# A new order for a two-block layer kernel: loads counted with a longer distance, VectorE's float32 copies kept apart from GpSimd, up to 200 planning rounds

## The chip, the cores and the metric

The kernel runs on one core of a Trainium2 chip. The metric is device time in microseconds (us) of one execution, the median of several runs. TensorE (PE in the profile), VectorE (DVE), ScalarE (ACT) and GpSimd (POOL) each work through a queue of instructions in order; SyncE (SP) issues all transfers between HBM and the on-chip memory SBUF, also in order. PSUM holds the results of matmuls, in 8 banks.

## What is computed

Two layers follow each other over 2048 tokens of width 1024, all in float32. Cut to what matters:

```python
def first_block(x, c, ...):
    shift, scale, gate = split(silu(c) @ ada_w + ada_b, 3)
    h = rmsnorm(x, norm_pre) * (1 + scale) + shift
    proj = h @ w_in                                   # 1024 -> 3072 columns
    attn = sliding_window_attention(q, k, v, sinks) * silu(ag)   # 8 heads, window 128
    rwkv = rwkv7_mixer(h, r, k, v, ...) * silu(rg)    # 4 heads, a recurrence over tokens
    gla = gla_mixer(h, gq, gk, gv, ...) * silu(gg)    # 4 heads, gated linear attention
    y = concat([attn, rwkv, gla]) @ w_out
    return x + gate * rmsnorm(y, norm_post)

def second_block(x, positions, ...):
    h = rms_norm(x, norm_g)
    q, k, v, qi, ki, wi, z_a, u_b, z_b, gates = split(h @ w_in_2)   # 1024 -> 4648
    # each query keeps the 256 best keys by an index score, then softmax over them
    a = dsa_attention(rope(q), rope(k), v, rope(qi), rope(ki), wi, 256) * silu(z_a)
    b = multiscale_pool(u_b, pool_w, pool_scale) * silu(z_b)
    g = sigmoid(gates + merge_bias)
    return x + (g[0] * (a @ w_branch_a) + g[1] * (b @ w_branch_b)) @ w_out_2

def reference(...):
    return second_block(first_block(x, c, ...), positions_2, ...)
```

## The kernel before

**Recording, then planning.** The program first writes down all work as a list of operations. A call such as `nc.vector.tensor_scalar(...)` issues nothing; `Plan.record` notes the operation, the memory that it reads and writes, and from these what it depends on. At the end `Plan.emit` asks `Plan.order` for one order of all operations and issues them in it. That is why every instruction of the profile has the same line, L414. The order fixes each engine's queue and SP's queue of transfers; at run time every engine works through its queue in order and waits for the data of the next instruction.

**The plan's rounds.** `order` starts from a rank for each operation: the length of the longest chain from it to the end. `forward` simulates the five queues: when an engine comes free, it takes the ready operation of highest rank (`walk`). `backward` does the same from the end, and gives new ranks. This goes on for at most `PASSES` rounds, or until `PATIENCE` rounds brought no shorter total; the order with the shortest planned total is kept.

**What the plan counts.** `price` gives the duration of an operation. A transfer is issued every 475 ns, starts 1125 ns after its issue or when the transfer before it is done, and lasts its bytes over 360 bytes per ns. `lag` is the distance from the end of an operation to the start of one that depends on it: some 100 to 240 ns between engines, 900 ns behind a transfer, 100 ns ahead of one. For two operations of one engine whose dependence carries no data it is 0.

**VectorE beside GpSimd.** `port` says of an operation whether VectorE or GpSimd holds the shared way into SBUF while it runs: before, the operations with two inputs in SBUF (`PAIRS`). `until` then lets a holding operation of VectorE start no earlier than 60 ns before the end of GpSimd's holding one, and any operation of GpSimd no earlier than 60 ns before the end of VectorE's. An operation whose start would be put off by more than `WAIT` (150 ns) is put aside for another ready one (`aside`).

**Movable operations.** Copies, scalings and sums in float32 have more than one way (`others`): a copy can run on ScalarE, VectorE or GpSimd. `forward` moves such an operation off its home engine if it is late and the other engine finishes it sooner.

**The work itself.** Tokens are held in four quarters of 512. Every float32 matmul with weights is split in three with high and low parts (`mm3`, `dense_s`). `weights` loads a 128x1024 block of raw weights (in_w_in, in_w_out and so on; 512 KB), splits it on ScalarE and GpSimd, and stores both parts in HBM (scr_w); later uses load the two parts again, 512 KB each. Two buffers of each part take turns. `dense` runs a list of weight tiles over one or two quarters. `mixers` holds the attention, RWKV and GLA work of one half of the tokens, which passes results through HBM (scr_am, scr_lt, scr_xt, scr_yT). `build_h` normalises rows of x or y: its two scalings per pair of rows are VectorE's 128x1024 float32 scalings. `out1`, `proj2_rows`, `topk`, `attn2` and `out2` are the later stages. Work without dependences between stages may run side by side, as the plan has it.

Of the kernel before, what the change touches and what calls it, by code (L numbers as in the profile page):

```python
# [8 lines left out]
F32 = mybir.dt.float32  # L9
F32R = mybir.dt.float32r  # L10
# [8 lines left out]
PSUM = bass.MemoryType.PSUM  # L19
# [18 lines left out]
EJ = ((2, "vector"), (3, "tensor"), (0, "tensor"), (1, "vector"))  # L38
B1, B2, B3, B4, B5 = 1, 1, 1, 1, 1
K0, K1, K2, K3, M0, M1 = 3, 4, 4, 4, 2, 2  # L40
PASSES, PATIENCE = 32, 12
SWITCH, NEAR, LOOK, WAIT, AHEAD = 90.0, 3000.0, 12, 150.0, 60000.0
FLEX, MARGIN, GAIN = 3, -10000.0, 500.0
ENGINES = ("tensor", "vector", "scalar", "gpsimd", "sync")
# [18 lines left out]
class Plan:  # L63
# [118 lines left out]
    def record(self, eng, name, args, kw):  # L182
        o = Op()
        o.eng, o.name, o.args, o.kw = eng, name, args, kw
        o.preds, o.succs, o.more = {}, [], set()
        i = len(self.ops)
        reads, writes = operands(name, args, kw)
        o.cost = price(eng, name, args, kw, reads, writes)
        o.ways = [(eng, name, args, kw, o.cost)]
        o.kind = kind(name, reads) if eng == "tensor" else None  # L190
        o.port = port(name, reads)
        for way in others(eng, name, args, kw, reads, writes):
            o.ways.append((*way, price(*way, reads, writes)))
        for aps, w in ((reads, False), (writes, True)):
            for ap in aps:
                r = self.region(ap)
                if r is not None:
                    self.touch(o, i, r, w and ap.tensor.name not in self.junk, ap.tensor.name)
        o.preds.pop(i, None)
        self.ops.append(o)  # L200
# [89 lines left out]

    def until(self, o, e, t):

        if e == "vector" and o.port:
            return max(t, self.held["gpsimd"] - 60.0)
        if e == "gpsimd":
            return max(t, self.held["vector"] - 60.0)
        return t
# [14 lines left out]
    def forward(self, rank, goal):  # L312

        ops = self.ops
        end, seq, dma = [0.0] * len(ops), [], [0.0]

        def take(i, e, t, now, avail, done):
            o = ops[i]
            free = self.until(o, e, t)
            if len(o.ways) > 1:  # L320
                mine = next(w for w in o.ways if w[0] == e)
                home = o.ways[0][0]
                if e != home:
                    slack = goal - rank[i] - t + MARGIN
                    if slack > 0:
                        return t + slack
                    w = o.ways[0]
                    start = max(now[home], t)
                    start += sum(ops[j].cost for r, j in avail[home] if -r > rank[i] and not done[j])
                    if start + w[4] <= t + mine[4] + GAIN:  # L330
                        return max(start + w[4] - mine[4] - GAIN, t + 50.0)
                o.eng, o.name, o.args, o.kw, o.cost = mine
            o.start = t
            if e == "sync":
                now[e] = t + 475
                dma[0] = o.end = max(dma[0], t + 1125) + o.cost
            else:
                now[e] = o.end = free + o.cost
                if o.port and e in self.held:
                    self.held[e] = o.end  # L340
                if e == "tensor":
                    if o.kind != self.kind:
                        now[e] = o.end = o.end + SWITCH
                    self.kind = o.kind
            end[i] = o.end
            seq.append(i)

        self.walk([len(o.preds) for o in ops],
                  lambda i: [(s, end[i] + lag(ops[i], ops[s], data)) for s, data in ops[i].succs], rank, take)
        return max(end), end, seq  # L350

    def backward(self, end):

        ops = self.ops
        tail, dma = [0.0] * len(ops), [0.0]
        ways = [o.ways for o in ops]
        for o in ops:
            o.ways = [(o.eng, o.name, o.args, o.kw, o.cost)]

        def take(i, e, t, now, avail, done):  # L360
            o = ops[i]
            if e == "sync":
                now[e] = t + 475
                dma[0] = max(dma[0], t) + o.cost
                tail[i] = dma[0] + 1125
            else:
                now[e] = tail[i] = self.until(o, e, t) + o.cost
                if o.port and e in self.held:
                    self.held[e] = tail[i]
                if e == "tensor":  # L370
                    if o.kind != self.kind:
                        now[e] = tail[i] = tail[i] + SWITCH
                    self.kind = o.kind

        self.walk([len(o.succs) for o in ops],
                  lambda i: [(p, tail[i] + lag(ops[p], ops[i], data)) for p, data in ops[i].preds.items()], end, take)
        for o, w in zip(ops, ways):
            o.ways = w
        return tail

    def order(self):

        ops = self.ops
        for i, o in enumerate(ops):
            for j, data in o.preds.items():
                ops[j].succs.append((i, data))
        rank = [0.0] * len(ops)
        for i in reversed(range(len(ops))):
            rank[i] = max((rank[s] + lag(ops[i], ops[s], data) for s, data in ops[i].succs), default=0.0) + ops[i].cost
        best, goal = None, math.inf  # L390
        stale = 0
        for k in range(PASSES):
            total, end, seq = self.forward(rank, goal)
            stale += 1
            if stale > PATIENCE:
                break
            if best is None or total < best[0]:
                stale = 0
                best = total, seq, [(o.eng, o.name, o.args, o.kw, o.cost, o.start, o.end) for o in ops]
            rank = self.backward(end)  # L400
            goal = total
            self.totals.append(total)
        self.total, self.seq, how = best
        for o, h in zip(ops, how):
            o.eng, o.name, o.args, o.kw, o.cost, o.start, o.end = h
        return self.seq
# [73 lines left out]
def operands(name, args, kw):  # L480

    reads, writes = [], []
    for i, x in enumerate(args):
        if is_ap(x):
            w = i == 0 or name == "tensor_tensor_reduce" and i == 7
            (writes if w else reads).append(x)
    for k, x in kw.items():
        if is_ap(x):
            (writes if k in ("out", "accum_out") else reads).append(x)
    return reads, writes  # L490
# [51 lines left out]
         "copy_predicated", "tensor_tensor_reduce"}  # L542


def port(name, reads):

    if name not in PAIRS:
        return False
    return all(reads[i].space != PSUM for i in (0, -1 if name == "scalar_tensor_tensor" else 1))


def kind(name, reads):


    if name == "transpose":
        return "transpose"
    return reads[0].dtype == F32R, reads[0].shape[0] == 128


def width(ap):  # L560
    n = 1
    for d in list(ap.shape)[1:]:
        n *= d
    return n
# [45 lines left out]
def lag(a, b, data):  # L610

    if a.eng == b.eng and not data:
        return 0.0
    if a.eng == "sync":
        return 900.0
    if b.eng == "sync":
        return 100.0
    return LAG[a.eng][b.eng]
# [1717 lines left out]
```

## Time and profile before

| | us |
|---|---|
| median of 3 runs | 3489.16 (3485.51 to 3496.49) |
| profiled execution | 3483.89 |
| its span, first to last instruction | 3482.1 |

The runs lie within 0.3% of each other. The profile comes from one execution; every stretch "A:B" below is in us from the start of its span. TensorE's mean granted clock in it was 0.956 of full speed.

### The profile page before, as it was taken

What the parts mean: (1) busy time and instruction counts of PE and PEld (TensorE: products, weight loads), DVE (VectorE), ACT (ScalarE), POOL (GpSimd) and SP (SyncE); (2) the same over time, 40 slices, a digit from 0 to 9 for tenths busy, and PEclk for the clock granted to TensorE, in tenths of its full rate; (3) what the DMA queues carried; (4) which work ended last, traced back from release to release, by engine and by line L of the source; (5) the groups of instructions that cost most, each with busy time, mean ns of one, the idle gap of its engine ahead of it and who ended that gap; (6) DMA issues with size and microseconds to landing.
All of it is one profiled execution on the core that took longest, in us unless ns stands there. A gap on an engine that the chain in (4) does not pass through costs nothing.

```text
span 3482.1 us, 53683 instructions
## 1 busy us (share of the span) xinstructions
PE 3165.3 (91%) x18258; PEld 2567.1 (74%) x18258; DVE 2399.1 (69%) x5421; ACT 1756.7 (50%) x3458; POOL 1336.7 (38%) x1379
## 2 busy tenths in 40 slices
PE   6899988998898999798999999999999988898988
PEld 5677666776666888787887777777777766777877
DVE  6367966666883656258878888789788687775442
ACT  3122225432123454257776767875786957446330
POOL 2232545441333554443323444353132236353421
PEclk7899989999998999999999999999999999899999
DMA  8477467547547888656644344362322346665656
GB/s 273 170 248 209 157 174 229 167 151 214 150 121 232 256 271 296 214 173 216 212 157 137 134 139 140 132 213 91 120 73 90 121 152 230 226 212 163 212 162 220
DMA packets 453961, 631.69 MB, mean 181 GB/s; under 512 B 83751, under 2 KB 309552, under 8 KB 453430
## 3 DMA queue, kind: packets, MB, share of 16 engines
q1 hardware_dynamic: 453686, 628.26, 56.1%
q8 instruction: 143, 2.34, 0.3%
q14 instruction: 132, 1.08, 0.1%
HBM read 397.31 MB, written 230.82 MB: 180 GB/s over the span
## 4 chain that ended last, share of the span: by engine, by line
PE 38%; DMA 13%; DVE 9%; ACT 6%; issue 4%; POOL 3%; SPq 1%; ACTq 0%; DVEq 0%; POOLq 0%
PE bank L414 38%; DVE arena L414 9%; DMA arena<-scr_w 6%; ACT arena L414 6%; POOL arena L414 3%; DMA arena<-in_w_in 1%; DMA arena<-in_w_out 1%; DMA out<-arena 1%; SPq L414 1%; DMA arena<-scr_y 0%; DMA arena<-scr_q 0%; DMA scr_x<-arena 0%; DMA arena<-scr_p_zb 0%; DMA arena<-in_w_branch_b 0%; DMA arena<-scr_yT 0%
## 5 line engine op out<-in xcount | busy, mean ns | idle before, releaser
L414 PE MATMUL bank<-arena 128*128 128x512 f32 (+8 forms) x18258 | 3165.3, 337 | 312.5 <-DVE arena L414 124.4
L414 PEld LDWEIGHTS bank<-arena 128*128 128x128 f32 (+3 forms) x18258 | 2567.1, 181 | 910.4 <-DVE arena L414 225.2
L414 POOL TENSOR_TENSOR arena<-arena 128x512 fp32r<-128x512 f32 (+16 forms) x1116 | 1240.1, 1127 | 1618.8 <-ACT arena L414 975.3
L414 ACT ACTIVATE arena<-arena 128x512 fp32r<-128x512 f32 (+32 forms) x1195 | 966.7, 824 | 804.4 <-DVE arena L414 421.1
L414 ACT ACTIVATE arena<-bank 128x512 f32<-128x512 f32 (+8 forms) x1423 | 724.4, 550 | 797.6 <-PE bank L414 649.9
L414 DVE TENSOR_TENSOR arena<-arena 128x512 fp32r<-128x512 f32 (+27 forms) x822 | 583.4, 724 | 209.3 <-ACT arena L414 103.6
L414 DVE SCALAR_TENSOR_TENSOR arena<-arena 128x512 f32<-128x512 f32 (+10 forms) x661 | 433.8, 661 | 59.5 <-POOL arena L414 19.3
L414 DVE TENSOR_SCALAR arena<-arena 128x1 f32<-128x1 f32 (+6 forms) x1129 | 272.8, 248 | 168.3 <-ACT arena L414 124.9
L414 DVE TENSOR_SCALAR_CACHE_REDUCE arena<-arena 128x384 int8<-128x384 bf16 (+13 forms) x238 | 351.3, 1476 | 11.9 <-ACT arena L414 6.8
L414 DVE CUSTOM_DVE_ANT_0 arena<-bank,arena 128x512 f32<-128x512 f32 (+3 forms) x448 | 251.7, 565 | 62.6 <-PE bank L414 60.6
L414 DVE TENSOR_TENSOR arena<-bank,arena 128x512 f32<-128x512 f32 (+3 forms) x170 | 95.4, 569 | 181.2 <-PE bank L414 144.3
L414 POOL TENSOR_SCALAR arena<-arena 128x4 f32<-128x4 f32 (+10 forms) x169 | 69.0, 409 | 327.9 <-DVE arena L414 159.1
L414 DVE SCALAR_TENSOR_TENSOR arena<-arena,bank 128x512 f32<-128x512 f32 (+1 forms) x264 | 127.5, 487 | 75.6 <-PE bank L414 42.4
L414 DVE COPY arena<-bank 128x512 f32<-128x512 f32 (+8 forms) x146 | 79.6, 548 | 114.9 <-PE bank L414 106.5
L414 ACT ACTIVATE arena<-bank,arena 128x512 f32<-128x512 f32 (+3 forms) x175 | 99.5, 579 | 65.0 <-PE bank L414 64.2
L414 DVE SCALAR_TENSOR_TENSOR arena<-bank,arena 64x64 f32<-64x64 f32 (+4 forms) x209 | 82.0, 393 | 63.1 <-PE bank L414 48.3
L414 ACT ACTIVATION_READ_ACCUMULATOR arena<-arena 128x1 f32 x590 | 114.9, 195 | 0.0
L414 POOL MEMSET arena<- 64x256 f32 (+7 forms) x69 | 21.8, 319 | 109.9 <-PE bank L414 57.6
L414 DVE CAST arena<-arena 128x512 fp32r<-128x512 f32 (+5 forms) x50 | 37.2, 751 | 24.2 <-PE bank L414 6.3
L414 DVE TENSOR_SCALAR arena<-bank 64x256 f32<-64x256 f32 (+2 forms) x44 | 18.0, 410 | 51.4 <-PE bank L414 47.0
L414 DVE TENSOR_TENSOR_SCAN arena<-arena 128x512 f32<-128x512 f32 (+14 forms) x26 | 53.1, 2041 | 0.2
L414 DVE TENSOR_REDUCE arena<-arena 128x1 f32<-128x3 f32 (+6 forms) x148 | 37.3, 252 | 9.5 <-ACT arena L414 8.1
(18 smaller groups left out, 215.7 us busy)
## 6 DMA issues: line engine op xcount, KB each, us to landing
arena<-scr_w SPq DMA_DIRECT2D x340, 512.0 KB
scr_w<-arena SPq DMA_DIRECT2D x174, 512.0 KB
arena<-in_w_in SPq DMA_DIRECT2D x52, 512.0 KB
arena<-in_x SPq DMA_DIRECT2D x32, 512.0 KB
scr_p_g<-arena SPq DMA_DIRECT2D x64, 256.0 KB
arena<-scr_p_g SPq DMA_DIRECT2D x64, 256.0 KB
arena<-in_ada_w SPq DMA_DIRECT2D x48, 256.0 KB
arena<-scr_p SPq DMA_DIRECT2D x16, 532.0 KB
```

What stands on the lines that cost most here:

```text
L414: ins = getattr(getattr(self.nc, o.eng), o.name)(*o.args, **o.kw)
```

## The change

Three things change in the plan, none in the list of operations.

Every operation that depends on a transfer is counted 2700 ns behind the transfer's end, 900 ns before. This holds for loads, and for stores whose tile is written anew or whose data is loaded again.

`port` is asked for each engine. For VectorE a `tensor_scalar` or `tensor_copy` with one output, wider than one element, with its first input and output in float32 in SBUF, now holds the shared way as well. It is asked with the name that the operation was recorded with: a ScalarE `activation` that the plan moves to VectorE as a copy is not counted.

The rounds go up to 200, and 30 may pass without a shorter total.

```diff
-PASSES, PATIENCE = 32, 12
+PASSES, PATIENCE = 200, 30
...
-        o.port = port(name, reads)
+        o.port = {e: port(e, name, reads, writes) for e in ("vector", "gpsimd")}
...
-        if e == "vector" and o.port:
+        if e == "vector" and o.port[e]:
             return max(t, self.held["gpsimd"] - 60.0)
...
-                if o.port and e in self.held:
+                if e in self.held and o.port[e]:
                     self.held[e] = o.end
...
-def port(name, reads):
+def port(eng, name, reads, writes):
     if name not in PAIRS:
-        return False
+        return eng == "vector" and name in ("tensor_scalar", "tensor_copy") and len(writes) == 1 and width(writes[0]) > 1 \
+            and all(x.space != PSUM and x.dtype in (F32, F32R) for x in reads[:1] + writes)
     return all(reads[i].space != PSUM for i in (0, -1 if name == "scalar_tensor_tensor" else 1))
...
     if a.eng == "sync":
-        return 900.0
+        return 2700.0
```

## Rows read from the trace of the kernel before

**Rows 1.** The page's first lines: span; busy us, share, instructions of each engine.

```profile
span 3482.1 us, 53683 instructions
PE 3165.3 (91%) x18258; PEld 2567.1 (74%) x18258; DVE 2399.1 (69%) x5421; ACT 1756.7 (50%) x3458; POOL 1336.7 (38%) x1379
```

**Rows 2.** TensorE's waits, whole span: us in total, times, longest us.

```profile
PE bank L414 <- DVE arena L414: 124.4, 107, 10.1
PE bank L414 <- ACT arena L414: 78.6, 76, 6.1
PE bank L414 <- DMA arena<-scr_w: 73.7, 52, 11.0
PE bank L414 <- POOL arena L414: 26.2, 41, 1.7
```

**Rows 3.** The page's chain that ended last, by line, shares of the span.

```profile
PE bank L414 38%; DVE arena L414 9%; DMA arena<-scr_w 6%; ACT arena L414 6%; POOL arena L414 3%; DMA arena<-in_w_in 1%; DMA arena<-in_w_out 1%; DMA out<-arena 1%; SPq L414 1%; DMA arena<-scr_y 0%; DMA arena<-scr_q 0%; DMA scr_x<-arena 0%; DMA arena<-scr_p_zb 0%; DMA arena<-in_w_branch_b 0%; DMA arena<-scr_yT 0%
```

**Rows 4.** TensorE's waits for stored weights: 348:1740, then 2784:3482.

```profile
PE bank L414 <- DMA arena<-scr_w: 49.9, 27, 11.0
...
PE bank L414 <- DMA arena<-scr_w: 19.2, 18, 2.4
```

**Rows 5.** Timeline of TensorE: start, us, first of the merged, [idle before, releaser].

```profile
862.15 18.04 PE L414 MATMUL bank<-arena 128*128 128x512 f32 x80 [4.40 <-DMA arena<-scr_w]
...
887.12 13.05 PE L414 MATMUL bank<-arena 128*128 128x512 f32 x45 [4.88 <-DMA arena<-scr_w]
...
1067.89 12.36 PE L414 MATMUL bank<-arena 128*128 128x512 f32 x43 [10.97 <-DMA arena<-scr_w]
...
1437.07 3.33 PE L414 MATMUL bank<-arena 128*128 128x256 f32 x14 [9.59 <-DMA arena<-scr_w]
...
3444.30 15.95 PE L414 MATMUL bank<-arena 128*128 128x256 f32 x131 [0.70 <-DMA arena<-scr_w]
```

**Rows 6.** Loads in the chain, from issue to use: start us, us, what.

```profile
987.57 6.53 DMA arena<-scr_w
...
1427.23 9.70 DMA arena<-scr_w
...
2640.86 4.25 DMA arena<-scr_w
...
3436.53 7.63 DMA arena<-scr_w
```

**Rows 7.** Timeline of SP's queue ahead of the load at 1061.67.

```profile
1050.53 0.41 SPq L414 DMA_DIRECT2D scr_yT<-arena  x1
...
1061.67 0.92 SPq L414 DMA_DIRECT2D arena<-scr_w  x2
```

**Rows 8.** Slices of 10 us: length, each engine's busy us, granted clock, DMA share, GB/s.

```profile
1060.00:1070.00 10.00, 2.11 (x4) 1.34 (x5) 0.00 (x0) 0.00 (x0) 0.00 (x0) 0.52 0.92 284
1070.00:1080.00 10.00, 10.00 (x40) 7.42 (x40) 4.47 (x12) 2.77 (x5) 1.28 (x1) 0.80 0.57 196
```

**Rows 9.** Timeline of VectorE and GpSimd; then groups by form: busy us, mean ns.

```profile
1279.54 0.75 DVE L414 TENSOR_SCALAR arena<-arena 128x1024 f32<-128x1024 f32 x1
1280.81 4.46 POOL L414 TENSOR_TENSOR arena<-arena 128x512 fp32r<-128x512 f32 x2 [3.44 <-ACT arena L414]
1283.20 2.62 DVE L414 TENSOR_SCALAR arena<-arena 128x1024 f32<-128x1024 f32 x1 [1.37 <-DMA scr_x<-arena]
...
2460.08 0.48 DVE L414 TENSOR_SCALAR arena<-arena 128x512 f32<-128x512 f32 x1 [0.48 <-PE bank L414]
...
L414 DVE TENSOR_SCALAR arena<-arena 128x512 f32<-128x512 f32 x67 | 41.4, 628 | 22.1 <-ACT arena L414 18.6 <-PE bank L414 2.1 <-DMA arena<-in_ada_w 1.0
L414 DVE TENSOR_SCALAR arena<-arena 128x1024 f32<-128x1024 f32 x30 | 30.1, 1017 | 13.4 <-POOL arena L414 9.0 <-DMA scr_x<-arena 4.3
```

**Rows 10.** SP's waits on TensorE (total us, times, longest); the page's DMA issues.

```profile
SPq L414 <- PE bank L414: 900.4, 376, 20.3
...
arena<-scr_w SPq DMA_DIRECT2D x340, 512.0 KB
```

More of the change, by code (lines that the diff above doesn't have):

```diff
@@ L367, in take @@
                 now[e] = tail[i] = self.until(o, e, t) + o.cost
-                if o.port and e in self.held:
+                if e in self.held and o.port[e]:
                     self.held[e] = tail[i]
```

## The prediction

> **What bounds the kernel now.** I read the busy times first, then TensorE's waits, the chain that ended last, the waits cut by stage, and at last single stalls. The busy times show one engine that is nearly full: TensorE works 3165.3 us of a span of 3482.1 us, VectorE 2399.1 us and the others less [rows 1]. So only TensorE's idle time, some 317 us, and the reduced clock in part of its work can be won by another order. The waits say who ends this idle time: VectorE 124.4 us, ScalarE 78.6 us, stored weights coming back from HBM (scr_w) 73.7 us, GpSimd 26.2 us [rows 2]. The change speaks to the third directly, to the others only through the order. The chain by line, which can be followed back to 927 us, agrees: behind TensorE (38%) and VectorE (9%) stand the stored-weight loads with 6%, some 209 us of the span, and first-time weight loads (in_w_in, in_w_out) with 1% each [rows 3]. Time in the chain is no idle time of TensorE: most of each load runs beside matmuls.
>
> By stage, 49.9 us of the 73.7 us lie between 348 and 1740 us (mixers beside dense layers), 19.2 us from 2784 us to the end [rows 4] and the remaining 4.6 us in the attention stage between. The first stretch is lumpy. Four waits, of 4.40, 4.88, 10.97 and 9.59 us, are 29.84 us of its 49.9 us [rows 5]; the other 23 average 0.87 us.
>
> **The change part by part.** Every instruction is taken from the same recorded list with the same data dependences. No wait and no DMA is added; what moves is the order on each of the five queues, and for some movable copies the engine. So no duration is removed: the change is worth what the new order does to waits.
>
> *Loads.* The plan counts a 512 KB load as 1.125 us + 524288/360 = 1.456 us + 0.9 us = 3.48 us from issue to user, on an idle queue; after the change 5.28 us. The chain holds 34 pieces of scr_w; of these the shortest is 4.25 us, the longest 9.70 us, the first 6.53 us, the last 7.63 us [rows 6]; and 6% of the span over 34 is a mean of 6.1 us [rows 3]. The old count is below even the shortest piece; the new one lies between the shortest and the mean. So the old plan put users too early on TensorE's in-order queue, and matmuls that were ready stood behind them. With 1.8 us more per load it should place such matmuls first, or send the load sooner.
>
> What that is worth, per wait: no more than the 1.8 us that the plan newly sees. Between 348 and 1740 us that is 20.06 us of short waits plus 4 x 1.8 = 7.2 us, 27.3 us; attention 4.6 us; the end at most 19.2 us, where 18 waits average 1.07 us [rows 4]. To use it there must be other matmuls. In the first stretch mixers and dense layers run side by side, so I take three quarters: 20 us. At the end one stream of weights runs through two buffers with little beside it: half, 9 us. Attention: 2 us. Sum 31 us. Of the four long stalls another 29.84 - 7.2 = 22.6 us is not explained by 1.8 us; they are accidents of the order. At 1061.67 us SP sent the load only after a crowd of small attention loads that began to form at 1050.53 us behind a store of yT [rows 7], while TensorE stood still for 10.97 us [rows 5]. A new order deals these anew; I take a third, 8 us. Bounds for the whole part from below and above: 0 us, if nothing else is ready, to 73.7 us.
>
> A stall also costs clock. In the slice with the 10.97 us wait the granted clock is 0.52, and in the next one, with TensorE busy all 10 us, 0.80, so part of it at the lower of the clock's two levels [rows 8]: 2.0 us of full-speed work lost in that slice after an 11 us stall, near 0.2 us per us. On 31 + 8 = 39 us that is 8 us more, with 0 as the lower bound.
>
> First-time weight loads reach TensorE through ScalarE and GpSimd, whose waits on it are 78.6 and 26.2 us [rows 2]. The lines in_w_in and in_w_out are 2% of the chain together against 6% of scr_w [rows 3], so by share a third of 39 us at most, 13 us; a longer way leaves less of it on TensorE, and I take 4 us.
>
> A rule speaks against this. The Trainium skill, DMA: Bandwidth & Descriptors, "Anatomy of one DMA", fits one DMA's time as 2.0 us plus bytes over 436 GB/s, which is an estimate of 3.2 us for 512 KB on the other kind of DMA queue. By it the old 3.48 us was already enough, and the loads' part of the sum would be 0; the 4.25 to 9.70 us of the chain speak against using it here.
>
> *VectorE's copies.* The plan may no longer put a float32 copy or scale of VectorE in SBUF over a GpSimd instruction. The trace shows the collision: alone, a 128x1024 scale took 0.75 us, and the one started while GpSimd was in two subtractions (1280.81 us, 4.46 us long) took 2.62 us [rows 9]. The means over the kernel are 1017 ns for 30 of that size and 628 ns for 67 of 128x512, which takes 0.48 us alone [rows 9]: 30 x 0.27 + 67 x 0.15 = 18 us of VectorE's time. That is the gain's upper bound; few of these stand in front of TensorE, so I take 3 us. Copies that the plan moved over from ScalarE keep their old name in it and are not counted, so their collisions stay. From the other side, GpSimd is planned later behind such copies; were TensorE's waits on GpSimd to double, 26 us would be lost [rows 2].
>
> *Rounds.* Up to 200 instead of 32, and 30 without progress instead of 12. They cost no time on the chip. What they buy cannot be read from the trace, since the order kept is the one that the plan itself holds best. Nearest rows for a bound: all waits of TensorE on other engines, 229 us [rows 2]; an order that brings a tenth of them back or adds a tenth is worth 23 us either way. I take 0.
>
> *What is late next.* Where a load no longer ends a wait, a computing engine will in part: these ended 229.2 us of waits against 73.7 us by stored weights [rows 2]. I take a third of the 39 us as passed on: +13 us.
>
> Sum: -39 - 8 - 4 - 3 + 13 = -41 us. The profiled execution took 3483.89 us (its span 3482.1 us, 1.8 us around it), so 3443 us; its time is 5.3 us below the median of the runs, 3489.16 us. Between 3443 us and 3448 us I take 3446 us. The edge of "no change" is 0.3%, 10.5 us.
>
> **The rivals.**
> 1. *SP's queue becomes the bottleneck (slower).* SP issues in order and waits for whatever the next DMA needs: on TensorE alone 900.4 us in 376 waits [rows 10]. If the longer count only moves loads ahead in that queue, before their buffer is free, then SP stands at them 1.8 us longer: 340 stored-weight loads [rows 10] x 1.8 us = 612 us, with stores and small loads queued behind. If a tenth reaches TensorE that is +61 us in place of the give-back of 13: 3443 - 13 + 61 = 3491 us in the profiled execution, 3496 us as a median; if 15% does, 3527 us. It decides from (41 + 13)/612, about 9%. For it: the stall at 1061.67 us began with SP held by a store [rows 7]. Against it: all loads get the same surplus, so loads keep their order among themselves.
> 2. *No cover (no change).* Loads are sent when a buffer comes free, and no other matmuls are ready. At 3436.53 us a load went out and was used 7.63 us later [rows 6]; TensorE waited just 0.70 us for it [rows 5], so the buffers already hide most. Then only chance is left: 3480 us, within 10 us or so. The 3.2 us estimated by the Trainium skill's DMA: Bandwidth & Descriptors belong to this case: by them the surplus is slack.
> 3. *The whole order gets better.* Truthful loads, truthful copies and more rounds take half of all 303 us of waits that rows 2 list, less the usual give-back of a third: -101 us, and clock with it (0.2 x 101 = 20 us): 3363 to 3385 us.
> 4. *GpSimd pushed back (slower).* Its waits double, +26 us, and no load gain: 3510 us.
>
> **How the numbers follow.** Forecast (3415 to 3475 us) 0.52; rival 1 0.15; rival 2 0.16; rival 3 0.12; rival 4 0.05. Faster by over 0.3%: nearly all of the forecast (0.50), rival 3 (0.12), a quarter of rival 2 (0.04), 0.66. Slower: rival 4, two thirds of rival 1, a fifth of rival 2, 0.19. Within 0.3%: the rest, 0.15. The range takes in the forecast, rival 2, the better part of rival 1 and the near end of rival 3: 3383 to 3508 us.
>
> **What would show it.** Right: TensorE's waits on scr_w fall from 73.7 to 40 us or less, the waits over 4 us between 850 and 1440 us are gone, that stretch's clock rises, and TensorE's waits on engines stay near 229 us. The load pieces of the chain keep their 4 to 10 us; only what lies beside them changes. Right for the copies: the means of 1017 and 628 ns fall towards 750 and 480 ns. Wrong: scr_w waits as before (rival 2); SP's waits on TensorE well over 900 us and more TensorE waits on engines (rival 1); waits on GpSimd doubled (rival 4). Most of all it would be wrong if the new order brings a few stalls of 5 to 10 us of its own, for four such made up 30 us here.

## The result

The changed kernel takes 3369.34 us (median; 3365.47 to 3384.78) against 3492.82 us for the kernel before beside it: a ratio of 0.9651, interval 0.961 to 0.9693. It is 3.5% faster. The forecast was 1.2% and its range ended at 3383 us: the direction was right, the size a third of what came.

The changed kernel's page, first lines (span; busy us, share, instructions by engine):

```profile
span 3363.6 us, 53567 instructions
PE 3127.1 (93%) x18258; PEld 2558.4 (76%) x18258; DVE 2393.6 (71%) x5415; ACT 1758.5 (52%) x3470; POOL 1346.2 (40%) x1373
```

Set beside [rows 1], the span is 118.5 us shorter. TensorE's idle time (span less busy) went from 316.8 to 236.5 us, which is 80.3 us; the other 38.2 us are TensorE's own busy time, for the same 18258 matmuls. The other engines work as long as before.

TensorE's waits in the changed kernel, whole span, and below them its waits on stored weights from 336 to 1682 us and from 2691 us to the end, the same stages as in [rows 4] by the count of matmuls (us in total, times, longest):

```profile
PE bank L414 <- DVE arena L414: 113.8, 103, 11.5
PE bank L414 <- ACT arena L414: 59.8, 73, 4.7
PE bank L414 <- POOL arena L414: 32.1, 49, 3.4
PE bank L414 <- DMA arena<-scr_w: 17.4, 18, 3.7
...
PE bank L414 <- DMA arena<-scr_w: 15.4, 15, 3.7
...
PE bank L414 <- DMA arena<-scr_w: 2.1, 3, 1.6
```

The reader is to see two falls. Stored weights went from 73.7 us in 52 waits [rows 2] to 17.4 us in 18, and the longest from 11.0 to 3.7 us; at the end of the kernel, where 18 waits took 19.2 us [rows 4], three are left with 2.1 us. And the waits on the three computing engines, which the forecast had growing, fell from 229.2 to 205.7 us.

The busy time fell as well, and the granted clock rose. The groups of matmuls by form, 128x512 in the kernel before and then in the changed one (busy us, mean ns; idle before):

```profile
L414 PE MATMUL bank<-arena 128*128 128x512 f32 x6986 | 1888.8, 413 | 148.3 <-DMA arena<-scr_w 46.6 <-ACT arena L414 46.5 <-DVE arena L414 38.4
```

```profile
L414 PE MATMUL bank<-arena 128*128 128x512 f32 x6986 | 1854.3, 409 | 87.6 <-ACT arena L414 33.2 <-DVE arena L414 31.0 <-DMA arena<-scr_w 11.0
```

The same 6986 matmuls are busy for 34.5 us less, and the idle time before them fell by 60.7 us. The mean granted clock rose from 0.956 to 0.968 between these two executions; 3165.3 x 0.956 = 3026 and 3127.1 x 0.968 = 3027, so the fall of busy time has the size of the rise of the clock. That the two agree so closely is in part luck: over the 18 profiles of this document the same product runs from 3005 to 3044 us. The profiled execution of the kernel before also had a low clock for that kernel: 38 of its executions had 0.952 to 0.966, with a median of 0.960, and the four of the changed kernel 0.964 to 0.969. From the medians, 0.960 and 0.9675, some 24 us would be the clock's share, by estimate.

The page's chain that ended last, by line, and then VectorE's scalings by form, both of the changed kernel:

```profile
PE bank L414 47%; DVE arena L414 14%; ACT arena L414 6%; POOL arena L414 4%; DMA arena<-scr_w 2%; DMA out<-arena 1%; DMA arena<-in_w_in 1%; SPq L414 1%; DMA arena<-scr_p_za 1%; DMA arena<-scr_yT 0%; DMA arena<-in_x 0%; DMA arena<-in_w_out 0%; DMA arena<-scr_p 0%; DMA arena<-scr_y 0%; DMA arena<-scr_am 0%
```

```profile
L414 DVE TENSOR_SCALAR arena<-arena 128x512 f32<-128x512 f32 x67 | 39.1, 594 | 18.1 <-ACT arena L414 15.6 <-PE bank L414 1.9
L414 DVE TENSOR_SCALAR arena<-arena 128x1024 f32<-128x1024 f32 x25 | 21.1, 856 | 8.3 <-POOL arena L414 6.7 <-DMA scr_x<-arena 1.6
```

Stored-weight loads fell from 6% of the span [rows 3] to 2%, though the chain is followed further back here, to 490 us instead of 927 us. For that reason the larger shares of TensorE and VectorE can't be compared with [rows 3] as they stand. VectorE's scalings of 128x1024 went from 1017 to 856 ns and those of 128x512 from 628 to 594 ns [rows 9].

### The profile page after: what moved, and what is told of

The parts are those of the page before. It is cut to its first block, busy times and chain, and to the rows that moved or that the text cites. A ratio compares the mean times of both kernels' runs of the same rounds, so it can differ in the third digit from the quotient of the medians.

```text
span 3363.6 us, 53567 instructions
## 1 busy us (share of the span) xinstructions
PE 3127.1 (93%) x18258; PEld 2558.4 (76%) x18258; DVE 2393.6 (71%) x5415; ACT 1758.5 (52%) x3470; POOL 1346.2 (40%) x1373
## 4 chain that ended last, share of the span: by engine, by line
PE 47%; DVE 14%; DMA 9%; ACT 6%; issue 5%; POOL 4%; SPq 1%; DVEq 0%; ACTq 0%; POOLq 0%
PE bank L414 47%; DVE arena L414 14%; ACT arena L414 6%; POOL arena L414 4%; DMA arena<-scr_w 2%; DMA out<-arena 1%; DMA arena<-in_w_in 1%; SPq L414 1%; DMA arena<-scr_p_za 1%; DMA arena<-scr_yT 0%; DMA arena<-in_x 0%; DMA arena<-in_w_out 0%; DMA arena<-scr_p 0%; DMA arena<-scr_y 0%; DMA arena<-scr_am 0%
## 5 line engine op out<-in xcount | busy, mean ns | idle before, releaser
L414 PE MATMUL bank<-arena 128*128 128x512 f32 (+8 forms) x18258 | 3127.1, 335 | 232.3 <-DVE arena L414 113.8
L414 POOL TENSOR_TENSOR arena<-arena 128x512 fp32r<-128x512 f32 (+14 forms) x1118 | 1262.4, 1145 | 1482.7 <-ACT arena L414 773.1
L414 ACT ACTIVATE arena<-arena 128x512 f32<-128x512 f32 (+31 forms) x1207 | 971.9, 822 | 739.0 <-DVE arena L414 451.1
L414 ACT ACTIVATE arena<-bank 128x512 f32<-128x512 f32 (+9 forms) x1420 | 719.3, 547 | 740.2 <-PE bank L414 632.7
L414 DVE TENSOR_TENSOR arena<-arena 128x512 f32<-128x512 f32 (+30 forms) x820 | 603.3, 749 | 179.7 <-ACT arena L414 90.9
L414 DVE TENSOR_SCALAR arena<-arena 128x1 f32<-128x1 f32 (+8 forms) x1120 | 252.6, 233 | 161.7 <-ACT arena L414 130.2
L414 DVE CUSTOM_DVE_ANT_0 arena<-bank,arena 128x512 f32<-128x512 f32 (+3 forms) x448 | 251.2, 566 | 60.9 <-PE bank L414 55.9
L414 POOL TENSOR_SCALAR arena<-arena 128x4 f32<-128x4 f32 (+8 forms) x161 | 56.6, 352 | 327.3 <-DVE arena L414 165.1
L414 DVE COPY arena<-bank 128x512 f32<-128x512 f32 (+7 forms) x136 | 74.1, 548 | 93.4 <-PE bank L414 83.2
L414 DVE SCALAR_TENSOR_TENSOR arena<-bank,arena 64x64 f32<-64x64 f32 (+4 forms) x209 | 81.8, 394 | 54.6 <-PE bank L414 37.7
L414 DVE CAST arena<-arena 128x1024 fp32r<-128x1024 f32 (+6 forms) x55 | 40.9, 749 | 15.4 <-POOL arena L414 4.3
L414 DVE CAST arena<-bank 128x512 fp32r<-128x512 f32 (+2 forms) x60 | 35.4, 594 | 15.6 <-PE bank L414 12.0
```

Of the source, the lines that this page charges most:

```text
L414: ins = getattr(getattr(self.nc, o.eng), o.name)(*o.args, **o.kw)
```

## The experiments

All times are medians; a ratio is to the kernel before, run beside. "Engines" is the sum of TensorE's waits on VectorE, ScalarE and GpSimd in the profile, "scr_w" those on stored weights, "busy" TensorE's busy time. Waits and busy time come from one execution of each kernel.

| kernel | us | ratio (interval) | scr_w | engines | busy |
|---|---|---|---|---|---|
| before | 3492.82 | 1 | 73.7 | 229.2 | 3165.3 |
| the change | 3369.34 | 0.9651 (0.961 to 0.9693) | 17.4 | 205.7 | 3127.1 |
| distance alone | 3366.85 | 0.964 (0.9615 to 0.9664) | 25.1 | 199.4 | 3126.7 |
| copies' count alone | 3459.26 | 0.9906 (0.9873 to 0.994) | 70.9 | 212.9 | 3149.5 |
| rounds alone | 3463.93 | 0.9924 (0.9895 to 0.9953) | 54.6 | 243.1 | 3147.4 |
| distance and rounds | 3369.74 | 0.9655 (0.9623 to 0.9686) | 28.3 | 201.6 | 3121.1 |
| 2700 ns for stored weights alone | 3451.87 | 0.9869 (0.9826 to 0.9912) | 32.0 | 253.4 | 3150.5 |
| 2700 ns for all but stored weights | 3428.85 | 0.9818 (0.979 to 0.9846) | 61.0 | 194.4 | 3157.6 |
| 2700 ns for loads | 3404.27 | 0.9751 (0.9719 to 0.9783) | 27.2 | 214.1 | 3129.7 |
| 2700 ns for stores | 3474.90 | 0.9948 (0.9928 to 0.9967) | 57.0 | 232.5 | 3177.9 |
| 880 ns | 3505.63 | 1.003 (1.0011 to 1.0049) | 89.7 | 234.3 | 3171.0 |
| 920 ns | 3471.94 | 0.9935 (0.991 to 0.996) | 66.2 | 233.4 | 3151.5 |
| 1800 ns | 3415.45 | 0.9783 (0.9755 to 0.9811) | 30.7 | 231.0 | 3145.6 |
| 2500 ns | 3384.68 | 0.9699 (0.9684 to 0.9713) | 31.4 | 212.2 | 3124.1 |
| 2900 ns | 3400.90 | 0.9747 (0.9732 to 0.9762) | 18.7 | 230.0 | 3135.1 |
| 3500 ns | 3400.88 | 0.9738 (0.9722 to 0.9755) | 18.4 | 219.9 | 3144.3 |
| 4500 ns | 3389.18 | 0.971 (0.9683 to 0.9737) | 8.2 | 222.8 | 3147.3 |
| the change, moved copies counted too | 3356.01 | 0.9614 (0.9594 to 0.9634) | 16.0 | 192.4 | 3128.1 |

**Which part does it.** The three parts one by one, on the kernel before.

```diff
     if a.eng == "sync":
-        return 900.0
+        return 2700.0
```

> The kernel before with the longer distance behind transfers alone (2700 ns for 900 ns). Theory A, the loads' distance is what pays: TensorE's waits on scr_w fall from 73.7 us to about 20 us, the granted clock rises from 0.956 to about 0.967, and the time falls by 80 to 120 us, to 3370 to 3410 us. Theory B, the search pays (more rounds): no more than 30 us here, 3460 to 3490 us, scr_w waits above 50 us. Theory C, any other order would do as well because the one of before was an unlucky draw: also some 3390 to 3420 us, but then the other parts alone bring the same.

Measured: 3366.85 us, scr_w waits 25.1 us, clock 0.967; the time is just below the range expected if the distance is what pays. The whole gain of the change comes with this one line.

The copies' count alone (the three edits of `port`, `until` and `held` as in the change, 900 ns and 32 rounds kept):

> The kernel before with the new count of VectorE's float32 copies alone. Theory A: within 20 us of before, 3470 to 3500 us, scr_w waits near 70 us; the means of VectorE's 128x1024 and 128x512 scalings fall from 1017 and 628 ns towards 860 and 590 ns as in the changed kernel. Theory C (a re-deal is enough): 3390 to 3440 us.

Measured: 3459.26 us, 0.9% faster, outside both ranges. The scr_w waits stayed, at 70.9 us. The 128x1024 scaling's mean is 980 ns, hardly better; that of 128x512 is 582 ns.

```diff
-PASSES, PATIENCE = 32, 12
+PASSES, PATIENCE = 200, 30
```

> The kernel before with up to 200 rounds and 30 without progress, nothing else. Theory A: within 20 us of before. Theory B: most of the gain, 3370 to 3420 us, with the clock at 0.965 or more. Theory C: 3390 to 3440 us.

Measured: 3463.93 us, 0.8% faster, again between the theories. More rounds on the old counts do not bring the gain.

Distance and rounds without the copies' count (the two small diffs above together):

> The changed kernel without the new count of VectorE's copies: longer distance and 200 rounds. Theory A: as the changed kernel within 20 us, 3360 to 3390 us, scr_w waits near 17 us. If the copies' count mattered as well, it is 20 to 40 us slower than the changed kernel, and the means of VectorE's 128x1024 scalings are back at 1000 ns.

Measured: 3369.74 us, the time of the whole change and of the distance alone. In the traces of this kernel and of the distance alone, every engine's instructions and SP's transfers stand in the same order from first to last, as far as the traces name them: the further rounds brought no other plan, so this is the same program run again. It shows how far one program's figures vary between executions: scr_w 25.1 and 28.3 us, engines 199.4 and 201.6 us, busy 3126.7 and 3121.1 us. On top of the distance the copies' count, which does give another order, isn't worth anything that these runs can tell.

**How much an order moves by chance.** A change of 20 ns carries no knowledge; it only deals the order anew.

```diff
-        return 900.0
+        return 880.0
```

> The kernel before with 880 ns in place of 900 ns behind transfers: a change of 20 ns that carries no better knowledge, so it only deals the order anew. If the order of before was a fair draw: 3475 to 3505 us. If it was an unlucky one, so that the 0.8 to 1.3% of the small changes so far were luck and not their doing: 3440 to 3470 us, with scr_w waits still at 55 to 75 us.

```diff
-        return 900.0
+        return 920.0
```

> The same with 920 ns. Together with 880 ns it gives the spread that the order alone makes: the theory of a fair draw wants the two on both sides of 3490 us or at it, that of an unlucky draw wants both at 3440 to 3470 us.

Measured: +0.3% and -0.65%, on both sides of before and each clear of it; 3505.63 us is just above the range for a fair draw, and 3471.94 us lies between the two ranges. By these two the order of before was no unlucky draw, and about half a per cent either way is chance. The 0.8 to 0.9% of the rounds and of the copies' count alone is little more than that, and is not shown to be their doing.

The nudge to 880 ns also shows what does not change with the draw. Its timeline of TensorE, three of its waits (start, us, form, [idle before, releaser]):

```profile
895.64 4.61 PE L414 MATMUL bank<-arena 128*128 128x512 f32 x10 [5.52 <-DMA arena<-scr_w]
...
1075.81 1.19 PE L414 MATMUL bank<-arena 128*128 128x512 f32 x2 [7.40 <-DMA arena<-scr_w]
...
1456.97 3.36 PE L414 MATMUL bank<-arena 128*128 128x256 f32 x14 [7.58 <-DMA arena<-scr_w]
```

These lie where three of the four long stalls lay before, at 887.12, 1067.89 and 1437.07 us [rows 5]. The nudge to 920 ns has two of them, 8.45 us at 1062.22 and 8.11 us at 1434.32 us. What the prediction called accidents of the order comes back in other orders made with the short distance.

**How long the distance should be.**

```diff
-        return 900.0
+        return 1800.0
```

> Half of the change in distance, 1800 ns behind all transfers, old count of copies, 32 rounds. If the plan pays by seeing the true load, with 6 us from issue to use in the chain: about half of the gain, 3410 to 3450 us, scr_w waits of 40 to 55 us. If any other order than that of before is as good: 3370 us too.

Measured: 3415.45 us, 2.2% faster, in the range expected, and scr_w waits already at 30.7 us, where 40 to 55 us were expected. The first 0.9 us of distance brings most.

The same line with 2500, 2900, 3500 and 4500 ns:

> The kernel before with 2500 ns behind all transfers, else as before. A neighbour of 2700 ns: if the 3.6% of the longer distance is its doing, 3355 to 3395 us; if a good part was a lucky draw at exactly 2700 ns, 3400 to 3430 us.

> The other neighbour, 2900 ns. The same two ranges: 3355 to 3395 us if the distance does it, 3400 to 3430 us if 2700 ns was lucky. The long stalls on scr_w near 870, 1060 and 1440 us, which every order made with 880 to 920 ns has had, should be gone or under 4 us in both.

> 3500 ns, so a 512 KB load counts 6.08 us, the mean that the chain of before shows. If the count is best where it is true to that mean: 3340 to 3370 us. If the gain is flat once the long stalls are gone: 3360 to 3395 us, with scr_w waits of 10 to 20 us.

> Past the change: 4500 ns, so a 512 KB load counts 7.08 us, more than the chain's mean of 6.1 us. If truth is what pays, then no further gain: 3360 to 3400 us, scr_w waits below 20 us but waits on engines up by 10 us or more. If a longer distance always helps (loads go out earlier): below 3350 us. If loads sent early hold up SP's queue: above 3400 us, with SP's waits on TensorE above 950 us.

Measured: 3384.68, 3400.90, 3400.88 and 3389.18 us. From 2500 to 4500 ns, 2700 ns included, the ratios are 0.9699, 0.964, 0.9747, 0.9738 and 0.971, a mean of 0.971 with no trend. So the distance is worth some 2.9%, and the order of 2700 ns alone is some 0.7% better than that; the range expected for a lucky draw at 2700 ns, 3400 us and above, holds at 2900 ns, but 2500 ns stays below it, in the range expected if the distance does it. 3500 ns, at 3400.88 us, missed both of its own ranges, which ended at 3395 us. With 2500 ns two long stalls are still there (TensorE's timeline):

```profile
1050.26 10.06 PE L414 MATMUL bank<-arena 128*128 128x512 f32 x29 [5.60 <-DMA arena<-scr_w]
...
1407.52 12.67 PE L414 MATMUL bank<-arena 128*128 128x256 f32 x87 [8.08 <-DMA arena<-scr_w]
```

yet the kernel is 3.0% faster, with 18 scr_w waits in all, not 52. The expectation that the stalls near those places would be gone in both neighbours failed at 2500 ns; most of the short waits went, and the gain came although two long ones stayed. With 4500 ns the scr_w waits are down to 8.2 us and the kernel is no faster than with 2500: the waits on engines are 222.8 us and TensorE's busy time is 3147.3 us. SP's own wait on TensorE, in the changed kernel and with 4500 ns:

```profile
SPq L414 <- PE bank L414: 885.4, 376, 18.1
```

```profile
SPq L414 <- PE bank L414: 937.3, 382, 14.4
```

It does rise at 4500 ns, by 37 us over before [rows 10], and nothing of the size of rival 1 follows from it. A nudge moves this sum more: with 880 ns it is 962.0 us.

**Which transfers.** First stored weights alone, then all transfers but these (`stored` looks whether the loaded tensor is one of scr_w):

```diff
     if a.eng == "sync":
-        return 900.0
+        return 2700.0 if stored(a) else 900.0
```

> The kernel before with 2700 ns behind the loads of stored weights (scr_w) alone, 900 ns behind all other transfers. If the stored weights carry the gain, as the sum in the prediction has it: waits on scr_w near 25 us, 3365 to 3410 us. If the gain comes from all transfers together (stores, raw weights, the passes of the mixers through HBM): scr_w waits fall but the time stays at 3430 us or above.

```diff
     if a.eng == "sync":
-        return 900.0
+        return 900.0 if stored(a) else 2700.0
```

> The reverse: 900 ns behind stored-weight loads, 2700 ns behind every other transfer. If the stored weights carry the gain: scr_w waits stay at 60 us or more (or rise, since other transfers now rank ahead of them) and the time stays at 3450 to 3495 us. If all transfers do: 3400 to 3440 us.

TensorE's waits with stored weights alone at 2700 ns (us in total, times, longest):

```profile
PE bank L414 <- DVE arena L414: 143.4, 97, 10.1
PE bank L414 <- ACT arena L414: 78.7, 79, 6.0
PE bank L414 <- DMA arena<-scr_w: 32.0, 17, 8.0
PE bank L414 <- POOL arena L414: 31.3, 45, 2.9
PE bank L414 <- DMA arena<-in_pool_w: 6.1, 2, 4.5
PE bank L414 <- DMA arena<-scr_p_av: 3.8, 1, 3.8
PE bank L414 <- DMA scr_p_ag<-arena: 3.0, 1, 3.0
```

and with all others at 2700 ns:

```profile
PE bank L414 <- DVE arena L414: 112.5, 106, 11.3
PE bank L414 <- DMA arena<-scr_w: 61.0, 49, 5.4
PE bank L414 <- ACT arena L414: 58.4, 55, 5.2
PE bank L414 <- POOL arena L414: 23.5, 32, 3.6
```

Measured: 3451.87 and 3428.85 us, 1.3% and 1.8% faster. This is the pair that tells most. With stored weights alone the waits on them fall by 41.7 us, nearly as far as in the change, but 19.0 us come back as waits on VectorE and 5.1 us on GpSimd, and waits on other transfers appear that were short or absent before: TensorE's idle time falls by 7.7 us only (3459.6 - 3150.5 = 309.1 us against 316.8 us). With all the others the waits on stored weights stay at 61.0 us, but the waits on engines fall by 34.8 us, and TensorE idles 269.4 us. The expectation that stored weights alone carry the gain is refuted: the other transfers, which seldom end a wait of TensorE themselves, bring at least as much, by way of TensorE's waits on the engines. Which of the two groups brings more is not shown, since 0.5% between two orders is no more than a nudge makes.

Loads against stores (a load is told by its target in SBUF):

```diff
     if a.eng == "sync":
-        return 900.0
+        return 2700.0 if a.args[0].tensor.name.startswith("arena") else 900.0
```

> 2700 ns behind every load into SBUF, 900 ns behind stores to HBM. If all loads together are the cause: 3365 to 3390 us, scr_w waits near 25 us. If the passes through HBM matter (a store followed by a load of the same data, which the change counts twice longer): 3400 to 3440 us.

The reverse, with the two numbers exchanged:

> 2700 ns behind stores to HBM alone, 900 ns behind loads. If all loads together are the cause: 3440 to 3490 us, no better than a nudge, scr_w waits at 55 us or more. If the passes through HBM matter: 3400 to 3440 us.

Measured: 3404.27 us and 3474.90 us, 2.5% and 0.5% faster. The loads bring most of it, though 3404.27 us lies in the range expected if the passes through HBM matter. The stores' half per cent is no more than a nudge's; whether they add to the loads, whose 2.5% is 1.1% short of all transfers at 2700 ns but level with 2900 and 3500 ns, stays open.

**A version that is faster still.** The changed kernel counts a copy by the name under which it was recorded. Here a way that the plan may choose is counted by its own name:

```diff
         for way in others(eng, name, args, kw, reads, writes):
             o.ways.append((*way, price(*way, reads, writes)))
+            if way[0] in o.port:
+                o.port[way[0]] = port(way[0], way[1], reads, writes)
```

> The changed kernel, and in addition the copies that the plan moves over from ScalarE count as holding VectorE's way to SBUF. If the collisions of VectorE's copies with GpSimd cost anything on the path that ends last: 3340 to 3360 us. If, as with the count of the other copies beside the longer distance, nothing comes of it: 3360 to 3385 us.

VectorE's casts in SBUF, which are the moved copies, in the changed kernel and then here (groups by form: busy us, mean ns):

```profile
L414 DVE CAST arena<-arena 128x1024 fp32r<-128x1024 f32 x24 | 18.1, 755 | 4.6 <-DMA arena<-in_w_in 3.9 <-PE bank L414 0.6
L414 DVE CAST arena<-arena 128x512 fp32r<-128x512 f32 x19 | 16.4, 870 | 5.6 <-DMA arena<-scr_yT 3.0 <-PE bank L414 1.7 <-DMA arena<-scr_h 0.5
```

```profile
L416 DVE CAST arena<-arena 128x1024 fp32r<-128x1024 f32 x9 | 6.2, 693 | 9.3 <-DMA arena<-in_w_out 8.0 <-DMA arena<-in_w_in 0.7 <-PE bank L416 0.6
L416 DVE CAST arena<-arena 128x512 fp32r<-128x512 f32 x10 | 5.9, 591 | 2.8 <-DMA arena<-scr_h 1.5 <-PE bank L416 0.7 <-POOL arena L416 0.6
```

Measured: 3356.01 us, the fastest of all, 3.9% below before. Of these two sizes 19 copies are moved instead of 43, and those that are run in 693 ns instead of 755 (128x1024) and 591 ns instead of 870 (128x512). That the 0.4% over the changed kernel comes from it is not shown: a nudge moves as much.

## Why the prediction fell short

**The mechanism was right.** The plan counted a transfer too short, TensorE stood in front of loads, and the longer count took these waits away; the distance alone, with nothing else changed, gives the time of the whole change. The loads themselves did not get faster. As far as the semaphore updates of the two traces let a load be followed (296 and 276 of the 340), a stored-weight load landed 5.4 us after its issue in the kernel before and 5.3 us in the changed one (medians), where the old plan counted 3.48 us and the new one 5.28 us. TensorE's first use of it moved from 6.9 to 8.0 us after the issue, and the loads used within 0.3 us of their landing fell from 103 to 54. Near the old stall at 1067.89 us, the longest, the changed kernel waits 1.95 us and, two matmuls later, 3.72 us, together 5.67 instead of 10.97:

```profile
1043.17 0.73 PE L414 MATMUL bank<-arena 128*128 128x512 f32 x2 [1.95 <-DMA arena<-scr_w]
1047.63 9.76 PE L414 MATMUL bank<-arena 128*128 128x512 f32 x41 [3.72 <-DMA arena<-scr_w]
```

**The loads' term was too small, and its step that failed is the cover.** It took three quarters of the short waits in the mixers, half at the end, and called the rest of the long stalls accidents, of which a third would go: 39 us. Measured: 56.3 us of 73.7. At the end, where I saw little beside one stream of weights, 17.1 of 19.2 us went. There was cover there, or the load could go out sooner; which of the two it was, no run here separates. And the stalls were no accidents: two nudges dealt the order anew and they came back. Nor did the cap of 1.8 us per wait hold: the longest stall lost 5.3 us.

**What is late next: +13 us was the wrong sign.** The waits on computing engines fell by 23.5 us. TensorE's waits on them in the mixers' stage, 348 to 1740 us before and 336 to 1682 us in the changed kernel:

```profile
PE bank L414 <- DVE arena L414: 50.6, 55, 3.8
PE bank L414 <- ACT arena L414: 29.5, 29, 4.5
PE bank L414 <- POOL arena L414: 9.9, 14, 1.7
...
PE bank L414 <- DVE arena L414: 58.7, 57, 6.1
PE bank L414 <- ACT arena L414: 24.2, 33, 2.5
PE bank L414 <- POOL arena L414: 11.6, 16, 3.4
```

Here 34.5 us of waits on stored weights went, and the waits on engines rose from 90.0 to 94.5 us: a give-back, but of an eighth, not a third. The fall lies elsewhere, 11.8 us ahead of this stage and 12.6 us in the attention stage, where stored weights had ended 4.7 us of waits in all. The pair of experiments shows why the step looked right: with stored weights alone counted longer, 24.2 of 41.7 us are indeed passed on to the engines. With every transfer counted longer, this part turns into a gain: the other transfers alone won 34.8 us of waits on engines. That the engines' own loads are placed better is likely but not settled: VectorE, ScalarE and GpSimd wait 566 us for transfers before and 417 us with all but stored weights at 2700 ns, but 511 us in the changed kernel, hardly less than the 519 us with 880 ns. I put a price on the transfers that end a wait of TensorE (and 4 us on first-time weights), and left out those that stand behind the engine that ends it.

**The clock's term was too small; by how much is less sure.** I took 0.2 us per us of idle time from the slice after the longest stall [rows 8], on 39 us: 8 us. Measured: 38.2 us of busy time against 80.3 us of idle time, 0.48 us per us, in one pair of executions of which the first had a low clock; by the median clocks it would be some 24 us, 0.3 us per us, by estimate. Other pairs with before give other values: 7.7 us against 47.4 with all but stored weights at 2700 ns, 17.9 against 73.3 with 4500 ns, 41.1 against 60.9 with 2500 ns. The first tenth of the span is not where it went: the granted clock rose there from 0.89 to 0.94, but the busy time ahead of the mixers' stage is 294.25 and 293.53 us. Mixers and attention have 16.7 and 16.5 us of the fall. One part of the miss is that twice as much idle time went as I had put down, which makes 16 us at 0.2 us per us; how much too low that price was, these runs do not settle.

Against the prediction's sum, by the terms of the trace: scr_w -56.3 us, engines -23.5, busy time -38.2, the rest -0.5; together -118.5 us, where -39, -4 - 3 + 13 = +6, and -8 stood.

**Copies: 3 us was fair.** The means fell (1017 to 856 ns, 628 to 594 ns), part of the way to the 750 and 480 ns named as the sign, and with or without the count the time is the same within 1 us (3369.34 and 3369.74 us). With the distance alone, and no count of copies, they are 983 and 600 ns, so of the smaller size most of the fall is not the count's doing. The Trainium skill, SBUF — State Buffer, "Who interferes with whom", says that copies, casts and scalings of VectorE can enter modes in which it takes the ports that it shares with GpSimd, and that whoever issues first then has them for the whole instruction. The casts of 128x512, at 591 ns where they are kept apart and 870 ns in the changed kernel, agree with it. Whether that lies on the path the runs must say, and no gain of time is shown here.

**Rounds: 0 us was right.** With the longer distance they brought no other order, and with the old one 0.8%, little more than a nudge.

**The rivals.** Rival 3 had the size (3363 to 3385 us) and half of the cause, truthful loads; copies and rounds, which it also named, did not contribute measurably. Rival 1 fails: the kernel is faster, and SP's waits on TensorE fell from 900.4 to 885.4 us. That sum decides little by itself, for the fastest kernel of all has 939.2 us. Rival 2 fails: counts of 1800 ns and more behind the transfer, 4.4 us and up for 512 KB, gain 2.2 to 3.6%. By the estimate of 3.2 us from the Trainium skill, DMA: Bandwidth & Descriptors, "Anatomy of one DMA", whose fit is for the other kind of DMA queue, they would be slack. The loads of this trace took longer, 5.4 us in the median. Rival 4 fails: waits on GpSimd rose by 5.9 us, not by 26. The risk named last, new long stalls, looks as if it had come true: at 1391.30 us TensorE now waits 6.13 us for VectorE. But that stall is an old one. It stands ahead of the same matmul by count, the 7437th, as the 9.59 us at the old 1437.07 us [rows 5], and two matmuls later come 1.13 us on stored weights. In all 18 kernels TensorE stands still there for 7 to 10 us, behind stored weights or VectorE or both; the change took 2.3 us off it and handed most of the rest to VectorE.

```profile
1391.30 0.69 PE L414 MATMUL bank<-arena 128*128 128x128 f32 x2 [6.13 <-DVE arena L414]
1393.12 7.08 PE L414 MATMUL bank<-arena 128*128 128x256 f32 x44 [1.13 <-DMA arena<-scr_w]
```

The luck of the draw may be in the result as well: by the five distances from 2500 to 4500 ns a fair value is 2.9%, so some 0.6 of the 3.5% may belong to this one order. It is not shown, since three different orders made with 2700 ns, those of the change, of the distance alone and of the faster version, all gained 3.5 to 3.9%, more than any of the other four distances; two of these three count the copies as well.

## What to carry to other kernels

Where a planner orders the queues, compare its count for a transfer with the pieces of the chain, and correct it for every transfer at once: correcting only the loads that end TensorE's waits passed more than half of the gain on to other waits. Judge any change of a planned order against two or three nudges that mean nothing; here they moved the time by +0.3% and -0.65%, so a single order that is 0.5% better shows little. And price idle time of TensorE with its clock, but from more than one profile: in the kernels here in which over 40 us of idle time went, each us took another 0.2 to 0.7 us of busy time with it.

## What was not expected of the hardware

The mean granted clock of one and the same kernel differs from one execution to the next: in 38 executions of the kernel before it ran from 0.952 to 0.966, while the time stayed between 3479 and 3508 us. So the busy time of a single profile, 3121.1 to 3177.9 us over these kernels for the same 18258 matmuls, is no measure of an order by itself: the 3177.9 us, with 2700 ns for stores, come from an execution at 0.952, and the other seven of that kernel had 0.956 to 0.965.
